# Transfers in source order through the scan and output stages of a parallel-head layer

## The chip, the cores and the metric

The kernel runs on one core of a Trainium2 chip. The metric is the device time of one execution in microseconds (us); lower is better. Several executions are timed and the median is taken; one more execution is profiled, and every row below comes from that one. Engines are named as in the profile: PE multiplies matrices (PEld are its weight loads), DVE, ACT and POOL work on vectors, and SP issues the DMA transfers of this kernel from one in-order queue.

## What is computed

One layer of a diffusion backbone for 128 context tokens and 2048 latent tokens (T = 2176), width 1024, all in float32. The layer normalises and modulates x, projects it, runs a short gated convolution on one half of the channels and a bidirectional mLSTM scan (4 heads of 128) on the other, projects back, adds to x, and ends with a feed-forward part. Cut to what this change touches:

```
h = rmsnorm(x, norm1) * (1 + scale1) + shift1
z = h @ w_in                                   # sc_b, sc_c, sc_x, q, k, v, o, gates
y_sc = sc_b * conv3(sc_c * sc_x)               # short gated convolution
h_m, C, n, m = mlstm_bidir(q, k, v, gates, C0, n0, m0)   # chunks of 128 tokens, two directions
h_m = h_m * rsqrt(mean(h_m**2) + EPS) * mh_norm * sigmoid(o)
x = x + gate1 * (concat(y_sc, h_m) @ w_out)
h2 = rmsnorm(x, norm2) * (1 + scale2) + shift2
up = conv3(h2 @ w_up); a, gg = split(up)
x = x + gate2 * ((silu(gg) * a) @ w_down)
y = rmsnorm(x, final_norm)
```

## The kernel before

Activations lie channels on partitions, tokens along the row. The 2176 tokens are cut into six blocks (BL), five of 384 and one of 256 tokens; blocks 0, 1, 2 are BA, blocks 3, 4, 5 are BB. Every float32 operand of a product is split into a rounded part and a remainder (names ending in H and L, or wh and wl), and a tile of a product takes three matmuls per 128 channels: `gemm` (L201) issues 24 of them, eight each at L206, L207, L208, into one of three accumulator banks. `load_w` (L107) brings a weight tile of 512 KB into a staging tile (`wst`, two buffers, L109), ACT makes wh (L111) and DVE makes wl in two halves (L114); wh and wl have four buffers.

`apply` (L168) normalises and modulates one block: `spread` (L134) puts the per-token factor on all partitions in the one PSUM bank `st`, then for each of eight tiles DVE multiplies (L177), ACT adds the shift and rounds (L181, L185, L186), and DVE forms the remainder (L182, L187). Three pairs of h buffers rotate over the blocks.

The stages, in source order:

1. Start: modulation, block 3, then value and gate products (`vg`, L378) and all projections of BB. With the o projection of BB by block, the h of blocks 0, 1 and 2 is made, each after the four heads that free its buffer (L624 to L626).
2. `vg` of BA (L926): for each block two halves of the columns, three chunks each, 24 matmuls per group (L388 to L390); ACT writes the values (L393), DVE adds the gate bias (L395), which is the last reader of the accumulator. Then the gate phase, woven with the k heads.
3. The scan, in two runs of `weave` (L909). `Sums` units collect state sums per chunk and head pair, `Mix` units compute the outputs. In iteration i the loop traces the first part of unit i, the third part of unit i-3, the second part of unit i-1, the loads of unit i+2, and then one or two steps of a generator `fill` (none in some iterations). The fill (L948) is a chain: q heads and o heads of BA (12 steps each), the short convolution of BA (36 steps), and the output projection of block groups (0, 1) and (2, 3) (16 steps each).
4. What is left of the fill, the sums for the feed-forward part, the output projection of blocks 4 and 5, and the feed-forward part.

In `heads` (L406) a step is one gemm, its eviction by ACT (L403) and the store of the row (L404); the first statement for each head is `load_w`, traced in the step of that head's first block. In `shortconv` (L420) the three weights of a channel tile are loaded in the step of its first gemm; each third step stores a row (L444). In `out_proj` (L451) the two blocks of a group are loaded and split at the group's start (L459 to L462), then for each of eight tiles and each of the two blocks: gemm, DVE multiplies by the gate and adds x (L488), the row is stored (L490), ACT squares it (L497), DVE adds the square up one step later (L498). At the group's end `inv_rms` (L122) sums over partitions with small matmuls (L128) in the bank `st`, DVE scales (L131), POOL takes the power (L132).

In a Mix unit the second product operand R is a 512 KB broadcast from DRAM (L839). The first part multiplies q and k into the one bank S (L850), DVE adds the mask to R (L851), ACT takes exponentials (L855), DVE multiplies S and R (L859), which frees S. The second part loads o2 (L770 via L864), multiplies with the state and values (L873, L875). The third part transposes into the bank `st` (L902), DVE multiplies with o2 (L904), which frees the bank, and o2 is stored (L907). Unit loads are k and q (L770), v (L775), R and sb (L843).

What sets the order on each engine is the planner of the tile framework. It takes the program in source order, simulates it with its own cost model, and issues on each engine what is ready first there, the earlier in the source first among the ready. So a load can be issued long before the place in the source where it is written, as soon as a buffer is free. The finished queue of each engine runs strictly in order on the chip, SP's too.

Of the kernel before, what the change touches and what calls it, by code (L numbers as in the profile page):

```python
# [2 lines left out]

# [7 lines left out]
F32 = mybir.dt.float32  # L11
# [46 lines left out]
def hymba_kernel(ctx: ExitStack, tc: tile.TileContext, I, O):  # L58
# [92 lines left out]
    def rcol(b):  # L151
        t0, n = BL[b]
        return rc[:, t0 // P:(t0 + n) // P]
# [12 lines left out]
        return ss  # L166

    def apply(b, xt, norm):  # L168
        t0, n = BL[b]
        rb = spread(rcol(b), n)  # L170
        hH, hL = h_pair()
        sh = 0 if norm == 0 else 24
        for k in range(KT):
            x = xt[k // 4][:, k % 4]
            for a, e, v in spans(t0, t0 + n):
# [8 lines left out]
                else:  # L184
                    S.activation(x[:, a:e], x[:, a:e], AF.Identity, bias=sv)  # L185
                    S.activation(hH[:, k, a:e], x[:, a:e], AF.Copy)  # L186
                    V.tensor_sub(hL[:, k, a:e], x[:, a:e], hH[:, k, a:e].bitcast(F32))  # L187
        return hH, hL
# [8 lines left out]
    def accumulator():  # L197
        pool = pa[next(turn_a) % len(pa)]
        return pool.tile([P, 512], F32, name="acc")

    def gemm(w, h, n):  # L201
        (wh, wl), (hH, hL) = w, h
        acc = accumulator()
        for k in range(KT):
            w_h, w_l = wh[:, k * P:(k + 1) * P], wl[:, k * P:(k + 1) * P]
            PE.matmul(acc[:, :n], w_h, hH[:, k, :n], start=(k == 0), stop=False)  # L206
            PE.matmul(acc[:, :n], w_h, hL[:, k, :n], start=False, stop=False)  # L207
            PE.matmul(acc[:, :n], w_l, hH[:, k, :n], start=False, stop=(k == KT - 1))  # L208
        return acc


# [142 lines left out]
    with ExitStack() as ph1:  # L354
# [89 lines left out]
                    Q.dma_start(yD[m][:, t0:t0 + n], yr[:, :n])  # L444
                    yield

        def stats(grp, sss):
            for b, ss in zip(grp, sss):
                inv_rms(ss, BL[b][1], rcol(b))

        def out_proj(grps, defer=None):  # L451
            for grp in grps:
                ys, sss = [], []
                for b in grp:
                    t0, n = BL[b]
                    yH, yL = h_pair()
                    for kh in range(2):
                        yt = xp.tile([P, 4, 384], F32, name="xt")
                        Q.dma_start(yt[:, :, :n], yD[4 * kh:4 * kh + 4, :, t0:t0 + n].rearrange("k p t -> p k t"))  # L459
                        for k in range(4):  # L460
                            S.activation(yH[:, 4 * kh + k, :n], yt[:, k, :n], AF.Copy)
                            V.tensor_sub(yL[:, 4 * kh + k, :n], yt[:, k, :n], yH[:, 4 * kh + k, :n].bitcast(F32))  # L462
                    ys.append((yH, yL))
                    sss.append(ssp.tile([P, 384], F32, name="ss"))

                def load_r(m):
                    xs_ = []
                    for b in grp:
                        t0, n = BL[b]
                        xr = rp.tile([P, 384], F32, name="row")  # L470
                        Q.dma_start(xr[:, :n], I["x"][m][:, t0:t0 + n])
                        xs_.append(xr)
                    return xs_

                ws = [load_w(I["w_out"][m]) for m in range(2)]
                nx, pend = load_r(0), []
                for m in range(KT):
                    w, xs_ = ws.pop(0), nx
                    if m + 1 < KT:
                        nx = load_r(m + 1)  # L480
                    if m + 2 < KT:
                        ws.append(load_w(I["w_out"][m + 2]))
                    for b, y, ss, xr in zip(grp, ys, sss, xs_):
                        t0, n = BL[b]
                        acc = gemm(w, y, n)
                        for a, e, v in spans(t0, t0 + n):
                            a, e = a - t0, e - t0
                            V.scalar_tensor_tensor(xr[:, a:e], acc[:, a:e], modT[:, 16 + m, v:v + 1], xr[:, a:e],  # L488
                                                   op0=ALU.mult, op1=ALU.add)
                        Q.dma_start(xD[m][:, t0:t0 + n], xr[:, :n])  # L490
                        while pend:
                            pend.pop()()
                        if m == 0:
                            S.activation(ss[:, :n], xr[:, :n], AF.Square)
                        else:
                            sq = sqp.tile([P, 384], F32, name="sq")
                            S.activation(sq[:, :n], xr[:, :n], AF.Square)  # L497
                            pend.append(lambda ss=ss[:, :n], sq=sq[:, :n]: V.tensor_add(ss, ss, sq))  # L498
                        yield
                while pend:  # L500
                    pend.pop()()
                if grp is grps[-1] and defer is not None:
                    defer.append(lambda: stats(grp, sss))
                else:
                    stats(grp, sss)


        hs = {}
        with tc.tile_pool(name="start", bufs=1, side="right") as stp, \
# [316 lines left out]
        class Mix:  # L826
# [71 lines left out]
            def third(self):  # L898
# [7 lines left out]
                t0 = (c + 1) * P  # L906
                Q.dma_start(yD[4 + 2 * hp:6 + 2 * hp, :, t0:t0 + P].rearrange("h d t -> d h t"), o2)  # L907

        def weave(units, fill, blocks):  # L909

            n = len(units)
            for i in range(-1, n + 3):
                if 0 <= i < n:
                    units[i].first()
                if 0 <= i - 3 < n:
                    units[i - 3].third()
                if 0 <= i - 1 < n:
                    units[i - 1].second()
                for x in (0, 1) if i < 0 else (i + 2,):
                    if x < n:  # L920
                        units[x].load()
# [19 lines left out]
        for hp in range(2):  # L941
            sb = ml.tile([P, 2, 2, 129], F32, name="sb", bufs=5)
            Q.dma_start(sb[:, :, 1, :], I["state"][:, 1, 2 * hp:2 * hp + 2, :])
            sbs.append(sb)
            sf = mb.tile([P, 2, 129], F32, name=f"sf{hp}")
            Q.dma_start(sf, I["state"][:, 0, 2 * hp:2 * hp + 2, :])
            sfs.append(sf)
        fill = chain(heads(BA, hs, 12, qD, AF.Copy, QS), heads(BA, hs, 20, oD, AF.Sigmoid, 1.0),  # L948
                     shortconv(BA, hs), out_proj(((0, 1), (2, 3))))
# [11 lines left out]
        late = []  # L961
        last = out_proj(((4, 5),), late)
        run(islice(last, 1))
        for _ in sums(0, fpool, (1,), (6, 0)):
            run(islice(last, 1))
# [343 lines left out]
```

## Time and profile before

| | us |
|---|---|
| median of 3 runs | 2507.28 |
| the 3 runs | 2504.99, 2507.28, 2508.83 |
| the profiled execution | 2504.05 |
| its span, first to last instruction | 2502.2 |
| busy: PE | 2454.3 |
| busy: DVE | 1731.5 |
| busy: ACT | 1100.3 |
| busy: POOL | 62.9 |

The mean granted PE clock is 0.992 of full speed. Busy times are unions of an engine's instructions; matmuls overlap, so a busy PE is not PE at its peak, and the number of matmuls in a window says more. A wait is written as the waiting instruction, the one that released it, the total, the count and the longest. In rows of single instructions the first number is the start in us from the span's start, the second the duration; brackets hold the idle time of the engine before it and its releaser. SPq rows are DMA issues; the duration is that of the issue, and the landing comes later. By the map of the stages in time: value and gate products of BA begin at about 382 us, the scan's sums at about 500 us, its mixing at about 651 us, the output projection at about 835 us.

### The profile page before, as it was taken

How to read it: one execution, taken by the hardware profiler on the slowest of the kernel's cores; microseconds unless marked ns; L12 is line 12 of the kernel's file. 1: busy time of each engine (PE TensorE's matmuls, PEld its weight loads, DVE VectorE, ACT ScalarE, POOL GpSimd, SP SyncE). 2: the span in 40 equal slices, each digit the busy share in tenths (PEclk: the TensorE clock that was granted, in tenths of full speed). 3: DMA queues.
4: the chain of work that ended last, by engine and by line, in shares of the span. 5: the costliest groups of instructions: out<-in, count | busy, mean ns of one | idle time of the engine just before them, and what ended most of it. 6: DMA issues, size and time to landing. Idle time of an engine off the chain costs nothing.

```text
span 2502.2 us, 44204 instructions
## 1 busy us (share of the span) xinstructions
PE 2454.3 (98%) x17043; PEld 2398.2 (96%) x17043; DVE 1731.5 (69%) x3327; ACT 1100.3 (44%) x2109; POOL 62.9 (3%) x128
## 2 busy tenths in 40 slices
PE   8999999999999989999999999999999999999998
PEld 7999999999999989999999999999999988889998
DVE  4895443433467777789888888776767788677665
ACT  4511133333334444455455445554545454443343
POOL 0000000000011111000000000000000000000000
PEclk9999999999999999999999999999999999999999
DMA  8798723466567886877456446644454476576544
GB/s 276 264 288 257 251 93 112 136 204 205 183 198 213 250 276 198 279 253 259 149 196 217 144 161 212 219 147 168 146 168 147 164 269 233 191 272 207 183 154 151
DMA packets 252437, 506.18 MB, mean 202 GB/s; under 512 B 22962, under 2 KB 153154, under 8 KB 241346
## 3 DMA queue, kind: packets, MB, share of 16 engines
q1 hardware_dynamic: 252226, 503.35, 60.9%
q8 instruction: 134, 2.20, 0.4%
q14 instruction: 77, 0.63, 0.1%
HBM read 355.24 MB, written 148.03 MB: 201 GB/s over the span
## 4 chain that ended last, share of the span: by engine, by line
PE 79%; DMA 8%; DVE 8%; issue 1%; ACT 1%; SPq 1%; POOL 0%; DVEq 0%; ACTq 0%; POOLq 0%
PE pa L1148 7%; PE pa L1150 7%; PE pa L1149 7%; PE acc L206 6%; PE acc L208 6%; PE acc L207 6%; PE pb L1150 4%; PE pb L1148 3%; PE pb L1149 3%; DVE jk L560 3%; PE pa L1206 3%; PE pa L1207 3%; PE pa L1208 3%; DMA wD<-wm 2%; PE pc L1208 2%; PE pc L1206 2%
## 5 line engine op out<-in xcount | busy, mean ns | idle before, releaser
L206 PE MATMUL acc<-hH,wh 128*128 128x384 f32 (+1 forms) x1536 | 514.9, 335 | 5.5 <-DVE cr L430 4.1
L208 PE MATMUL acc<-hH,wl 128*128 128x384 f32 (+1 forms) x1536 | 505.9, 329 | 0.5 <-DVE wl L114 0.5
L207 PE MATMUL acc<-hL,wh 128*128 128x384 f32 (+1 forms) x1536 | 504.9, 329 | 0.0
L1148 PE MATMUL pa<-tH,wh 128*128 128x272 f32 x1408 | 408.5, 290 | 3.8 <-DVE row L488 2.7
L1150 PE MATMUL pa<-tH,wl 128*128 128x272 f32 x1408 | 407.2, 289 | 0.0
L1149 PE MATMUL pa<-tL,wh 128*128 128x272 f32 x1408 | 405.1, 288 | 0.0
L278 ACT ACTIVATE wh<-st 128x512 fp32r<-128x512 f32 (+1 forms) x312 | 189.0, 609 | 403.1 <-PE pa L1149 108.7
L206 PEld LDWEIGHTS acc<-hH,wh 128*128 128x128 f32 x1536 | 291.1, 190 | 8.0 <-DVE cr L430 4.7
L208 PEld LDWEIGHTS acc<-hH,wl 128*128 128x128 f32 x1536 | 290.9, 189 | 1.2 <-DVE wl L114 0.9
L207 PEld LDWEIGHTS acc<-hL,wh 128*128 128x128 f32 x1536 | 291.1, 190 | 0.7
L989 DVE SCALAR_TENSOR_TENSOR tt<-raw,fw,tt 128x127 f32<-128x127 f32 (+4 forms) x264 | 242.3, 947 | 49.3 <-ACT tt L995 48.2
L1148 PEld LDWEIGHTS pa<-tH,wh 128*128 128x128 f32 x1408 | 264.9, 188 | 4.8 <-DVE row L488 2.9
L279 DVE TENSOR_TENSOR wl<-st,wh 128x512 fp32r<-128x512 f32 (+1 forms) x312 | 205.4, 660 | 91.3 <-ACT wh L278 87.9
L1149 PEld LDWEIGHTS pa<-tL,wh 128*128 128x128 f32 x1408 | 265.4, 188 | 0.0
L1150 PEld LDWEIGHTS pa<-tH,wl 128*128 128x128 f32 x1408 | 264.7, 188 | 0.0
L1148 PE MATMUL pb<-tH,wh 128*128 128x272 f32 x704 | 203.6, 289 | 0.4 <-ACT wh L278 0.4
L1150 PE MATMUL pb<-tH,wl 128*128 128x272 f32 x704 | 203.6, 289 | 0.0
L1149 PE MATMUL pb<-tL,wh 128*128 128x272 f32 x704 | 202.7, 288 | 0.0
L278 ACT ACTIVATE wh<-s 128x512 fp32r<-128x512 f32 x176 | 110.9, 630 | 146.5 <-PE pc L1149 90.1
L114 DVE TENSOR_TENSOR wl<-wst,wh 128x512 fp32r<-128x512 f32 (+1 forms) x160 | 105.9, 687 | 64.2 <-ACT wh L111 64.2
L279 DVE TENSOR_TENSOR wl<-s,wh 128x512 fp32r<-128x512 f32 x176 | 120.7, 687 | 29.0 <-ACT wh L278 25.4
L1148 PEld LDWEIGHTS pb<-tH,wh 128*128 128x128 f32 x704 | 132.4, 188 | 0.6 <-ACT wh L278 0.6
(236 smaller groups left out, 5222.0 us busy)
## 6 DMA issues: line engine op xcount, KB each, us to landing
st<-in_w_up SPq DMA_DIRECT2D x88, 512.0 KB, 4.6
wst<-in_w_in SPq DMA_DIRECT2D x48, 512.0 KB, 4.1
wU<-s SPq DMA_DIRECT2D x22, 1024.0 KB, 6.5
s<-wU SPq DMA_DIRECT2D x22, 1024.0 KB, 5.7
st<-wD SPq DMA_DIRECT2D x32, 704.0 KB, 5.2
st<-in_w_down SPq DMA_DIRECT2D x28, 704.0 KB, 4.0
R<-nD SPq DMA_DIRECT2D x34, 512.0 KB, 5.4
wm<-in_w_modr SPq DMA_DIRECT2D x32, 512.0 KB, 3.7
```

Source lines behind the costliest of these rows:

```text
L114: V.tensor_sub(wl[:, a:a + n // 2], st[:, a:a + n // 2], wh[:, a:a + n // 2].bitcast(F32))
L206: PE.matmul(acc[:, :n], w_h, hH[:, k, :n], start=(k == 0), stop=False)
L207: PE.matmul(acc[:, :n], w_h, hL[:, k, :n], start=False, stop=False)
L208: PE.matmul(acc[:, :n], w_l, hH[:, k, :n], start=False, stop=(k == KT - 1))
L278: S.activation(wh[:, :n], a, AF.Copy)
L279: V.tensor_sub(wl[:, :n], a, wh[:, :n].bitcast(F32))
L989: V.scalar_tensor_tensor(o, i, w, o, op0=ALU.mult, op1=ALU.add)
L1148: PE.matmul(acc, wh[:, w], rh, start=(kk == 0 and i in (0, 1, 5)), stop=False, skip_group_check=True)
L1149: PE.matmul(acc, wh[:, w], rl, start=False, stop=False, skip_group_check=True)
L1150: mm = PE.matmul(acc, wl[:, w], rh, start=False, stop=(kk == 3), skip_group_check=True)
L1206: PE.matmul(acc[p], wh[:, k], th[:, t], start=(c == kk == 0), stop=False, skip_group_check=True)
L1208: PE.matmul(acc[p], wl[:, k], th[:, t], start=False, stop=(c == 2 and kk == nk - 1), skip_group_check=True)
```

## The change

- **Ties.** A context `queued()` notes the last SP instruction traced so far and, at its end, adds to each SP instruction traced inside it an ordering edge (no semaphore) behind that one. In `weave` three kinds of pieces run inside such a context: the first and third parts; the second part with the loads of unit i+2; each single step of the fill. The edges order the issue only, between pieces; within a piece the planner stays free. `heads` and `shortconv` themselves are not changed.
- **Output projection.** It becomes one sequence of 48 steps over three groups. Each group runs its first two tiles for the first block and then for the second, then tiles 2 to 5 in pairs, then the last two tiles for the first block and then for the second. `load_y` loads and splits one block in five portions, started at fixed steps: blocks 0 and 1 inside the short convolution, blocks 2 to 5 at output steps 4, 13, 23 and 30. `load_o` asks for the next output weight that is not loaded, when a weight has been used for the last time in a group. Rows of x are loaded three steps ahead.
- **Statistics.** `inv_rms` of a block is traced two steps after its last tile, its matmuls ordered behind the current gemm; only block 5 is left for later instead of blocks 4 and 5.
- **Third block.** The apply of block 2 becomes a generator that advances by one tile behind each value group of `vg`; its x tiles are loaded where the whole apply stood.

```diff
     def apply(b, xt, norm):
+        hH, hL = h_pair()
+        run(apply_to(hH, hL, b, xt, norm))
+        return hH, hL
+
+    def apply_to(hH, hL, b, xt, norm):
         t0, n = BL[b]
         rb = spread(rcol(b), n)
-        hH, hL = h_pair()
...
+            yield
...
+        GROUPS = ((0, 1), (2, 3), (4, 5))
+        STEPS = [(m, b) for a, z in GROUPS for m, b in
+                 [(0, a), (1, a), (0, z), (1, z)] + [(m, b) for m in range(2, 6) for b in (a, z)]
+                 + [(6, a), (7, a), (6, z), (7, z)]]
+        NEXT_Y = {4: 2, 13: 3, 23: 4, 30: 5}
...
+        def load_y(b):
+
+            t0, n = BL[b]
+            ys[b] = yH, yL = h_pair()
+            yt = []
+            for kh in range(2):
+                y = xp.tile([P, 4, 384], F32, name="xt")
+                Q.dma_start(y[:, :, :n], yD[4 * kh:4 * kh + 4, :, t0:t0 + n].rearrange("k p t -> p k t"))
+                yt.append(y)
+            yield
+            for k in range(KT):
+                y = yt[k // 4][:, k % 4, :n]
+                S.activation(yH[:, k, :n], y, AF.Copy)
+                V.tensor_sub(yL[:, k, :n], y, yH[:, k, :n].bitcast(F32))
+                if k % 2:
+                    yield
+
+        def load_o(x):
+            while x < len(STEPS) and STEPS[x][0] in wo:
+                x += 1
+            if x < len(STEPS):
+                wo[STEPS[x][0]] = load_w(I["w_out"][STEPS[x][0]])
...
+                while due and due[0][0] <= x:
+                    b1 = due.pop(0)[1]
+                    with tc.issue_after(latest[0].ins):
+                        inv_rms(sss[b1], BL[b1][1], rcol(b1))
...
+                if m == KT - 1:
+                    due.append((x + 2, b))
+                if b % 2:
+                    wo.pop(m)
+                    load_o(x + 1)
+                if x in NEXT_Y:
+                    prep = chain(prep, load_y(NEXT_Y[x]))
+                next(prep, None)
+                yield
...
-                hs[b] = make_h(b, I["x"], 0)
+                if b < 2:
+                    hs[b] = make_h(b, I["x"], 0)
+                else:
+                    hs[b] = h_pair()
+                    third = apply_to(*hs[b], b, load_x(b, I["x"], xp, "xt", 2), 0)
...
+        @contextmanager
+        def queued():
+
+            traced = nc.cur_bb.bb.instructions
+            n = len(traced)
+            last = next(i.name for i in reversed(traced) if i.engine == mybir.EngineType.SP)
+            yield
+            for i in traced[n:]:
+                if i.engine == mybir.EngineType.SP:
+                    tc.add_manual_dep(i, last, mybir.DependencyInfo(
+                        mybir.DependencyClass.NoSync, mybir.DependencyReason.DATA), reason="queued")
+
         def weave(units, fill, blocks):
 
             n = len(units)
             for i in range(-1, n + 3):
...
+                with queued():
+                    if 0 <= i < n:
+                        units[i].first()
+                    if 0 <= i - 3 < n:
+                        units[i - 3].third()
+                with queued():
+                    if 0 <= i - 1 < n:
+                        units[i - 1].second()
+                    for x in (0, 1) if i < 0 else (i + 2,):
+                        if x < n:
+                            units[x].load()
                 for _ in range(blocks[i % 3]):
-                    next(fill, None)
-
-
-        run(vg(BA, hs, load_vg(0) + load_vg(1)))
+                    with queued():
+                        next(fill, None)
+
+
+        run(vg(BA, hs, load_vg(0) + load_vg(1)), third)
+        run(third)
...
+        def before_out():
+
+            prep = iter(())
+            for x, _ in enumerate(shortconv(BA, hs)):
+                if x in (29, 32):
+                    prep = chain(prep, load_y((x - 29) // 3))
+                if x in (31, 34):
+                    load_o(0)
+                next(prep, None)
+                yield
+            run(prep)
+
         fill = chain(heads(BA, hs, 12, qD, AF.Copy, QS), heads(BA, hs, 20, oD, AF.Sigmoid, 1.0),
-                     shortconv(BA, hs), out_proj(((0, 1), (2, 3))))
+                     before_out(), islice(outs, 32))
```

More of the change, by code (lines that the diff above doesn't have):

```diff
@@ L207, in gemm @@
             PE.matmul(acc[:, :n], w_h, hL[:, k, :n], start=False, stop=False)
-            PE.matmul(acc[:, :n], w_l, hH[:, k, :n], start=False, stop=(k == KT - 1))
+            mm = PE.matmul(acc[:, :n], w_l, hH[:, k, :n], start=False, stop=(k == KT - 1))
+        latest[:] = [mm]
         return acc
@@ L445, in shortconv @@
                     yield
[L447 to L499, printed above, removed]
@@ L508, in hymba_kernel @@
+                if m == KT - 1:
[7 more added lines that the diff above has]
+                yield
+            while pend:
+                pend.pop()()
+            defer.append(lambda: [inv_rms(sss[b1], BL[b1][1], rcol(b1)) for _, b1 in due])
         hs = {}
@@ L960, in hymba_kernel @@
         fp = ph2.enter_context(tc.tile_pool(name="fp", bufs=1, side="right"))
-        late = []
-        last = out_proj(((4, 5),), late)
+        last = outs
         run(islice(last, 1))
```

49 lines of the change are left out of this document (35 added, 14 removed).

## Prediction

> **What bounds the kernel now.** I read the page first (engines, then DMA sizes), then the waits of TensorE (PE), then stage windows, and last the rows of single instructions.
>
> ```profile
> span 2502.2 us, 44204 instructions
> PE 2454.3 (98%) x17043; PEld 2398.2 (96%) x17043; DVE 1731.5 (69%) x3327; ACT 1100.3 (44%) x2109; POOL 62.9 (3%) x128
> wst<-in_w_in SPq DMA_DIRECT2D x48, 512.0 KB, 4.1
> R<-nD SPq DMA_DIRECT2D x34, 512.0 KB, 5.4
> ```
>
> PE is busy for 2454.3 of 2502.2 us. No edit here takes a matmul away, so whatever is won is PE idle time and the slow clock behind it; any new PE wait adds to the time at once. The profiled execution took 2504.05 us, 1.85 over its span and 3.2 below the median of 2507.28. The next two fences are the waits of PE and windows of 25 us (PE busy, weight loads, DVE, ACT, POOL, each with its count; then granted clock, DMA share, GB/s), with two long stretches last.
>
> ```profile
> PE S L850 <- DVE R L859: 5.1, 2, 4.6
> PE st L128 <- DVE o L904: 4.4, 1, 4.4
> PE acc L388 <- DVE gates L395: 3.9, 1, 3.9
> PE pa L1148 <- DVE row L488: 2.7, 1, 2.7
> ```
>
> ```profile
> 375.00:400.00 25.00, 21.06 (x157) 20.87 (x156) 17.18 (x36) 13.63 (x27) 0.30 (x3) 0.86 0.61 186
> 400.00:425.00 25.00, 25.00 (x209) 25.00 (x208) 1.74 (x11) 3.48 (x9) 0.81 (x8) 1.00 0.14 47
> 825.00:850.00 25.00, 25.00 (x168) 25.00 (x168) 21.65 (x60) 13.85 (x40) 4.12 (x6) 1.00 0.79 241
> 875.00:900.00 25.00, 20.36 (x130) 20.04 (x129) 19.51 (x59) 10.11 (x30) 2.40 (x4) 0.89 0.85 274
> 900.00:925.00 25.00, 25.00 (x160) 25.00 (x160) 16.57 (x50) 10.33 (x33) 3.31 (x6) 0.97 0.90 276
> 925.00:950.00 25.00, 20.44 (x101) 19.81 (x100) 17.43 (x55) 12.10 (x32) 4.22 (x6) 0.80 0.84 269
> 1075.00:1100.00 25.00, 21.77 (x164) 21.13 (x162) 17.00 (x29) 13.09 (x22) 1.92 (x2) 1.00 0.92 316
> 490.00:640.00 150.00, 149.76 (x844) 142.82 (x843) 51.91 (x116) 53.97 (x155) 0.00 (x0) 1.00 0.69 210
> ```
>
> Three waits of about 4 us carry the idle time that the change can touch, and each is followed by a lowered clock. The sums of the scan (490 to 640) are the opposite: 149.76 of 150 us busy, nothing to win, everything to lose.
>
> **What the three waits are worth.** *Value blocks (375 to 400).* 157 matmuls where the next window has 209: (209-157)/209 x 25 = 6.2 us lost, 3.9 idle and 2.3 slow clock. *L859 (875 to 925).* Against 168 matmuls, 130 and 160 are 5.7 + 1.2 = 6.8 us lost, 4.6 idle and 2.2 clock. *L904 (925 to 950).* Matmul records are missing, so I go by the clock: 0.80 over 25 us is 10 us at half speed, at most 5.0 lost, with 4.4 idle 9.4. With the second L850 wait (0.5) all that can go is 22.9 us. L1148 stands after the last output tile and stays.
>
> **Third block between value blocks.** The apply of block 2 (six spread matmuls, per tile a product L177, ScalarE copies and L187 or L182) leaves the head of the DVE queue and goes one tile behind each of the first eight value groups.
>
> ```profile
> 393.25 0.55 DVE L187 TENSOR_TENSOR hL<-xt,hH 128x384 fp32r<-128x384 f32 x1
> 393.72 0.70 DVE L114 TENSOR_TENSOR wl<-wst,wh 128x528 fp32r<-128x528 f32 x1
> 394.34 0.30 DVE L395 TENSOR_TENSOR gates<-acc,bgate 128x8 f32<-128x8 f32 x3
> ```
>
> Now three gate additions wait behind all of the apply and free three accumulators at once, at 394.34. After the change each comes behind one tile. The last half of a value weight (L114, to 394.42) is in the same queue and is needed by the fourth group, so I keep 1 us back: -5.2. The two x loads stay ahead of the value blocks. Block 2 is wanted by the thirteenth group, four groups after its last tile; that work covers the move.
>
> **Statistics, output blocks, output weights.** The statistics' matmuls (three per full block, as before) wait for the one st bank, which L904 reads. Now they stand straight behind the scan's matmuls; afterwards they follow an output tile's 24 matmuls, which are cover for L904; ss was finished a tile earlier. Their DVE scaling and POOL power move with them, and the sums that read the result come after the scan. I take the whole 9.4. The two loads, eight copies and eight subtractions per output block are the same work in four portions; output weights are still eight loads per group, now asked for about two tiles before use instead of when a buffer is free. That is near what a load needs (below), and missed in the four places inside the scan where a group begins or reaches its third weight: 0 to 3 us each, I take 2 in all.
>
> **Order on the transfer queue (SP).** In the output stage a broadcast R was issued at 886.71 and the DVE sat before the addition that reads it:
>
> ```profile
> 886.71 0.42 SPq L839 DMA_DIRECT2D R<-nD  x1
> 892.11 0.69 DVE L851 TENSOR_TENSOR R<-R,maskN 128x512 f32<-128x512 f32 x1 [4.50 <-DMA R<-nD]
> 892.72 0.74 DVE L488 SCALAR_TENSOR_TENSOR row<-acc,modT,row 128x128 f32<-128x128 f32 x2
> ```
>
> The eviction L488 and then L859 queued behind it. Tied, each R is issued two scan steps before use; DVE order is still the planner's, so of 6.8 + 0.5 I count 5.4. Together these edits give -5.2 - 9.4 - 5.4 + 2 = -18.
>
> Now the price. The ties hold for every fill in the scan, and there the weights of heads and short convolution are loaded by the same step that uses them (load_w as its first statement, no load ahead). Today the planner moves these loads forward:
>
> ```profile
> 499.72 0.33 SPq L109 DMA_DIRECT2D wst<-in_w_in  x1
> 511.01 0.37 SPq L770 DMA_DIRECT2D k<-kD  x1
> 513.10 0.40 SPq L775 DMA_DIRECT2D v<-vD  x1
> 527.66 1.06 ACT L111 ACTIVATE wh<-wst 128x1024 fp32r<-128x1024 f32 x1 [3.77 <-PE acc L207]
> ```
>
> Counted in order, the load issued at 499.72 is the one converted at 527.66: 28 us of lead. Tied, the load of the next head stands behind the row store (L404) of the last tile, and that store waits for the tile's matmuls and its eviction. SP holds everything behind it: the k and v of the coming unit, then the weight. PE's next tile waits for the weight.
>
> ```profile
> 491.23 0.49 ACT L403 ACTIVATE row<-acc 128x384 f32<-128x384 f32 x1 [4.54 <-PE acc L208]
> 491.75 0.33 SPq L404 DMA_DIRECT2D kD<-row  x1
> L114 DVE TENSOR_TENSOR wl<-wst,wh x36: 673/683/694, 498.4 to 783.7; 128x512 fp32r<-128x512 f32 x36
> 503.83 0.38 PE L792 MATMUL S<-ident,k 128*128 128x128 f32 x2
> 506.24 0.53 PE L206 MATMUL acc<-hH,wh 128*128 128x384 f32 x1
> ```
>
> Per head: eviction and store 0.85 (491.23 to 492.08), k and v 0.77, landing 4.1, conversion 1.06, first half of the remainder 0.68: 7.5 us. PE has scan units meanwhile; two of them fill 503.83 to 506.24, 2.4. That leaves 5 us, seven times (four q heads and four o heads, the first with nothing to wait for): 35.
>
> Four sets of short-convolution weights follow, three of them in the scan's second half, where the queue between a finished tile and a weight is longer:
>
> ```profile
> 678.02 0.33 SPq L444 DMA_DIRECT2D yD<-yr  x1
> 679.14 0.37 SPq L907 DMA_DIRECT2D yD<-o  x1
> 682.11 0.42 SPq L843 DMA_DIRECT2D sb<-sD  x1
> 675.12 0.60 PE L850 MATMUL S<-q,k 128*128 128x128 f32 x4
> 677.49 0.43 PE L206 MATMUL acc<-hH,wh 128*128 128x384 f32 x1
> ```
>
> From the tile's store (678.02) past the output store, R and the rest to the end of sb's issue are 4.5 us. Eviction 0.9, queue 4.5, landing 4.1, conversion 1.06 and 0.68 are 11.2, less one unit's 2.4 on PE: 8.8, or 7 where the next tile is in the same step; I take 8, four times: 32.
>
> All eleven outlast the 3.9 us after which the clock fell, so each costs 2.2 more (the two rows above): 24. Together 35 + 32 + 24 = 91, against 18 won: +73. 2504.05 + 73 = 2577, with 3.2 for the median **2580 us**.
>
> The bounds of one wait: low, two more units pulled forward make 2.6 per head, and below that length the clock held (the 2.7 us before L1148, clock 1.00 at 1075 to 1100); 5 per set with 1.7 of clock. 7 x 2.6 + 4 x 6.7 = 45, less 22.9: +22, 2529. High, the slowest exposed load:
>
> ```profile
> 669.71 0.33 SPq L109 DMA_DIRECT2D wst<-in_w_in  x1
> 676.50 1.04 ACT L111 ACTIVATE wh<-wst 128x1024 fp32r<-128x1024 f32 x1
> ```
>
> 6.8 instead of 4.1: 7 x 7.7 + 4 x 10.7 + 11 x 5 (the ten half-speed microseconds of 925 to 950) = 152, with 10 won: +142, 2649.
>
> The Trainium skill ("TensorE: Matmul & The Clock Gate", The HAM clock gate) states that about 3.4 us of idle halve the clock until a busy window of about 3.4 us has passed. By it a stall would cost 1.7 us of clock, 19 in all, and the time would be 2575; this trace's windows hold 7 and 10 us at half speed, so the rows go before the page.
>
> The Trainium skill ("DMA: Bandwidth & Descriptors", Anatomy of one DMA) also says that a transfer's semaphore wait takes place on the issuing sequencer before dispatch. It speaks against this change; in this trace L404 is issued within 0.03 us of its eviction's end, which agrees but does not prove it.
>
> **Rivals.** *The ties only cure.* If weights still arrive ahead, because the ties do not hold those loads back or the stores before them are never late, the three waits go and nothing comes: 2507 less 18 to 23, 2484 to 2489. For: the 28 us of lead. Against: the load is traced inside the tied step. It decides at a lead of 7.5 us before the previous head's last matmul. 0.11. *Scan units fill the waits*, the low bound: PE takes later units while it waits, 2520 to 2545. For: units need only k and v. Against: those are tied two steps ahead too. 0.15. *The queue is held longer*: of the three short-convolution loads the third waits for a staging buffer (two exist) and holds R and k behind it, so units stall too; above 2655. 0.05. *Neither*: gains and waits cancel within 0.2%, about what a measurement of this kernel can tell from no change. 0.03.
>
> **How the numbers follow.** Forecast 0.66, with 2545 to 2655. The range takes in the rival just below it: 2520 to 2655, 0.81. Faster is the first rival, 0.11; same 0.03; slower 0.66 + 0.15 + 0.05 = 0.86.
>
> **What would show it.** PE waits named L206 or L208 behind ACT wh L111 or DVE wl L114, about eleven, 4 to 9 us, between 500 and 780; clock near 0.9 in those windows; L109 issued right behind a row store; a conversion some 5 to 7 us after its issue, not 28. No waits L395 and L904 of 4 us. I am wrong if L109 keeps leads of 20 us or PE stays above 149 of 150 us busy in the scan's sums.

## The result and the profile after

The changed kernel is slower: 2589.88 us (median of 4 runs, 2586.94 to 2596.28) against 2506.14 us of the kernel before on the same chip (4 runs, 2504.01 to 2508.83). The ratio is 1.035, 95% interval 1.0324 to 1.0376. The forecast was 2580, range 2520 to 2655. The profiled execution of the changed kernel took 2592.02 us.

First the page of the changed kernel: the span, the busy engines, and the loads of projection weights and of R with the size of each and the median time (us) from issue to landing.

```profile
span 2590.1 us, 44059 instructions
PE 2489.3 (96%) x17043; PEld 2415.4 (93%) x17043; DVE 1736.2 (67%) x3327; ACT 1106.5 (43%) x2109; POOL 69.9 (3%) x128
...
wst<-in_w_in SPq DMA_DIRECT2D x48, 512.0 KB, 5.4
R<-nD SPq DMA_DIRECT2D x34, 512.0 KB, 5.4
```

The matmuls are the same 17043. The span is 87.9 us longer, PE's busy time 35.0; the rest, 52.9, is idle time. A busy time that grows with the same matmuls points to the clock: each lasts longer. The mean granted clock fell from 0.992 to 0.981. The share missing from full speed, 0.019 of 2590.1 us, less 0.008 of 2502.2 us before, gives an estimate of 29 us, most of the 35.0. Next the waits of PE in the changed kernel (total, count, longest).

```profile
PE acc L212 <- ACT wh L111: 31.7, 19, 6.4
PE y L836 <- DVE vw L829: 22.3, 13, 3.8
PE y L906 <- DVE hv L916: 3.0, 5, 1.4
```

L212 is the first matmul of `gemm` (L206 before). The waits at L395 and L904 that stood in this list before are gone, and so is the 4.6 us at L859. Two new ones lead: tiles that wait for their weight, as forecast, and scan units that wait for `vw`, the product made from a v that has just landed, which the forecast did not have. The sizes are not those of the forecast: only two of the waits for a weight are over 4 us (6.4 at 686.68 and 5.2 at 934.18), where about eleven of 4 to 9 us were expected. Three windows of the changed kernel follow (behind 500 us the same times no longer hold the same work as before):

```profile
375.00:400.00 25.00, 25.00 (x210) 25.00 (x209) 15.01 (x37) 12.15 (x26) 0.61 (x6) 1.00 0.58 189
525.00:550.00 25.00, 19.52 (x92) 16.80 (x91) 7.07 (x17) 6.70 (x19) 0.00 (x0) 0.86 0.38 114
490.00:640.00 150.00, 122.76 (x590) 107.36 (x588) 42.22 (x94) 40.37 (x111) 0.00 (x0) 0.90 0.46 139
```

The value blocks now run through (210 matmuls where 157 stood). The sums of the scan, 844 matmuls in 150 us before, hold 590: 122.76 us busy, and a clock of 0.90, which over 150 us is 30 us at half speed.

Where the 87.9 us lie can be read from stores that both kernels make: the last row of the first q head, the last row of the fourth o head, the last row of the short convolution, the last row of the output stage. Transfer issues of the kernel before, then of the changed one:

```profile
512.08 0.32 SPq L404 DMA_DIRECT2D qD<-row  x1
634.92 0.32 SPq L404 DMA_DIRECT2D oD<-row  x1
832.58 0.39 SPq L444 DMA_DIRECT2D yD<-yr  x1
1084.05 0.32 SPq L490 DMA_DIRECT2D xD<-row  x1
```

```profile
502.73 0.32 SPq L411 DMA_DIRECT2D qD<-row  x1
679.92 0.32 SPq L411 DMA_DIRECT2D oD<-row  x1
904.71 0.33 SPq L451 DMA_DIRECT2D yD<-yr  x1
1168.50 0.32 SPq L509 DMA_DIRECT2D xD<-row  x1
```

Seven heads took 122.8 us and take 177.2 (+54.4); the short convolution 197.7 and 224.8 (+27.1); the output stage 251.5 and 263.8 (+12.3); all else, span less these three, 1930.2 and 1924.3 (-5.9). The sum is 87.9.

What each stage lost shows in windows with the same bounds: heads, short convolution and output stage of the changed kernel, then the output stage of the kernel before.

```profile
502.73:679.92 177.19, 146.22 (x691) 127.92 (x689) 46.73 (x100) 45.52 (x123) 0.00 (x0) 0.88 0.44 134
679.92:904.71 224.79, 208.06 (x1278) 204.55 (x1277) 129.53 (x392) 83.75 (x241) 22.43 (x36) 0.96 0.60 184
904.71:1168.50 263.79, 243.50 (x1528) 239.15 (x1526) 195.25 (x530) 121.65 (x302) 26.67 (x37) 0.96 0.82 265
```

```profile
832.58:1084.05 251.47, 238.98 (x1517) 237.13 (x1515) 188.96 (x519) 114.02 (x292) 22.13 (x36) 0.97 0.82 259
```

PE is idle for 31.0 us in the heads and for 16.7 in the short convolution (before, for 0.0 in both), and for 20.3 in the output stage (before 12.5). All 22.3 us of the waits behind vw lie in the heads. The waits for weights, in the heads and then in the output stage:

```profile
PE acc L212 <- ACT wh L111: 4.5, 7, 0.9
```

```profile
PE acc L212 <- ACT wh L111: 16.6, 7, 5.2
```

So of the 31.7 us that tiles wait for weights only 4.5 lie in the heads. There PE waits mostly in scan units.

How one head loses its time, from the timeline of the changed kernel:

```profile
502.21 0.49 ACT L410 ACTIVATE row<-acc 128x384 f32<-128x384 f32 x1 [3.90 <-PE acc L214]
502.73 0.32 SPq L411 DMA_DIRECT2D qD<-row  x1
503.14 0.39 SPq L803 DMA_DIRECT2D k<-kD  x1
503.63 0.43 SPq L854 DMA_DIRECT2D sD<-sb  x1
504.12 0.42 SPq L808 DMA_DIRECT2D v<-vD  x1
504.59 0.44 SPq L109 DMA_DIRECT2D wst<-in_w_in  x1
...
509.24 1.11 PE L836 MATMUL y<-vw,kT 128*128 128x258 f32 x4 [2.51 <-DVE vw L829]
510.12 1.05 ACT L111 ACTIVATE wh<-wst 128x1024 fp32r<-128x1024 f32 x1
...
511.22 0.69 PE L212 MATMUL acc<-hH,wh 128*128 128x384 f32 x1 [0.88 <-ACT wh L111]
```

The eviction of the head's last tile (502.21) releases the row store, and behind it in the queue go k, the state store, v, and only then the weight. 9.0 us after the eviction's start PE begins the next tile. It took scan units meanwhile, but their v (504.12) stood behind the same store, and so PE waited 2.51 us inside the cover too.

### The profile page after: what moved, and what is told of

Same layout as the page of the kernel before. It is cut to its first block, busy times and chain, and to the rows that moved or that the text cites. A ratio compares the mean times of both kernels' runs of the same rounds, so it can differ in the third digit from the quotient of the medians.

```text
span 2590.1 us, 44059 instructions
## 1 busy us (share of the span) xinstructions
PE 2489.3 (96%) x17043; PEld 2415.4 (93%) x17043; DVE 1736.2 (67%) x3327; ACT 1106.5 (43%) x2109; POOL 69.9 (3%) x128
## 4 chain that ended last, share of the span: by engine, by line
PE 74%; DMA 11%; DVE 8%; ACT 2%; issue 2%; SPq 2%; POOL 1%; DVEq 0%; ACTq 0%; POOLq 0%
PE pa L1211 7%; PE pa L1213 7%; PE pa L1212 7%; PE acc L212 6%; PE acc L213 5%; PE acc L214 5%; PE pb L1213 3%; PE pb L1211 3%; PE pb L1212 3%; PE pa L1269 2%; PE pa L1270 2%; PE pa L1271 2%; DVE jk L589 2%; DMA wD<-wm 2%; PE pc L1211 2%
## 5 line engine op out<-in xcount | busy, mean ns | idle before, releaser
L212 PE MATMUL acc<-hH,wh 128*128 128x384 f32 (+1 forms) x1536 | 521.0, 339 | 36.8 <-ACT wh L111 31.7
L213 PE MATMUL acc<-hL,wh 128*128 128x384 f32 (+1 forms) x1536 | 512.5, 334 | 0.0
L212 PEld LDWEIGHTS acc<-hH,wh 128*128 128x128 f32 x1536 | 298.5, 194 | 45.1 <-ACT wh L111 38.7
L213 PEld LDWEIGHTS acc<-hL,wh 128*128 128x128 f32 x1536 | 297.0, 193 | 0.3 <-issue 0.2
```

## Experiments

The table gives each kernel's median, its ratio to the kernel before with the 95% interval (the kernel before, timed beside them, had medians of 2503.2 to 2504.6), and the stage times of its profiled execution, read from the same four stores (us). One execution can lie some us off the median (4.3 below it in 7, 6.7 above it in 10), so stage differences of that size say little.

| | median | ratio | heads | short conv. | output | all else |
|---|---|---|---|---|---|---|
| before | | | 122.8 | 197.7 | 251.5 | 1930.2 |
| after | 2589.88 | 1.035 (1.0324 to 1.0376) | 177.2 | 224.8 | 263.8 | 1924.3 |
| 1 weights untied | 2501.27 | 0.9987 (0.9973 to 1.0001) | 124.6 | 201.6 | 249.8 | 1926.0 |
| 2 only weights tied | 2510.44 | 1.0024 (1.0009 to 1.0040) | 122.9 | 209.2 | 251.6 | 1923.0 |
| 3 weights earlier | 2515.73 | 1.0044 (1.0031 to 1.0058) | 122.4 | 208.9 | 260.9 | 1925.2 |
| 4 output weights too | 2511.53 | 1.0021 (1.0010 to 1.0032) | 122.4 | 209.8 | 252.3 | 1924.9 |
| 5 k and v untied | 2525.00 | 1.0087 (1.0070 to 1.0105) | 122.0 | 225.3 | 255.9 | 1920.7 |
| 6 ties alone | 2611.23 | 1.0432 (1.0410 to 1.0455) | 174.9 | 225.2 | 271.5 | 1936.7 |
| 7 no ties | 2496.23 | 0.9974 (0.9963 to 0.9985) | 122.8 | 198.4 | 247.4 | 1921.6 |
| 8 third block alone | 2498.34 | 0.9981 (0.9970 to 0.9993) | 122.8 | 197.3 | 249.6 | 1925.8 |
| 9 no ties, own bank | 2495.66 | 0.9964 (0.9952 to 0.9976) | 122.8 | 199.1 | 249.4 | 1923.5 |
| 10 and a fifth R | 2490.49 | 0.9954 (0.9937 to 0.9970) | 122.8 | 198.3 | 244.6 | 1929.6 |
| 11 third block, own bank | 2498.37 | 0.9976 (0.9964 to 0.9988) | 122.8 | 198.3 | 252.9 | 1924.8 |
| 12 third block, fifth R | 2500.69 | 0.9990 (0.9976 to 1.0004) | 122.8 | 198.5 | 251.5 | 1928.5 |

**1. Weight loads without ties.** `load_w` notes its transfers, and `queued` leaves them out:

```diff
-        Q.dma_start(st[:, :n], src)
+        wst_loads.add(Q.dma_start(st[:, :n], src).ins.name)
...
-                if i.engine == mybir.EngineType.SP:
+                if i.engine == mybir.EngineType.SP and i.name not in wst_loads:
```

> The changed kernel with one thing undone: the loads of weight tiles (load_w, in the fill of the scan) carry no ordering edge, all other transfers keep theirs. My theory (the price is the weight loads tied behind the row stores of the tiles before them): the TensorE waits of gemm behind ACT wh and DVE wl between 500 and 1100 us go, those of the scan units behind vw with them, and 90 to 105 us of the 2590 go: 2485 to 2505, the head's load issued over 20 us before its conversion. Rival A (the price is the ties on the scan units' own loads, k, v, R and o2 held behind stores): nothing changes there, above 2560. Rival B (the price is the new output stage itself): the 25 to 30 us lost after 900 us stay, 2515 or more.

Measured 2501.27: 88.6 of the 2589.88 us go with this one class of transfer. Heads are back at 124.6, while k and v keep their ties there. In this kernel's window of the sums PE is busy again, at full clock:

```profile
490.00:640.00 150.00, 148.66 (x837) 141.32 (x836) 52.74 (x116) 58.22 (x151) 0.00 (x0) 1.00 0.64 194
```

Its waits of PE name neither wh L111 nor vw. So the waits for v were a consequence: the units came under PE early only because the weight was missing. Rivals A and B fall. (At the few steps whose last transfer is a weight load, three-weight steps of the short convolution and output steps, the pieces behind it are tied to a free load; the heads have no such step.)

**2. Only the weight loads tied.** The complement:

```diff
+                if i.engine == mybir.EngineType.SP and i.name in wst_loads:
```

> The complement of the kernel with untied weights: only the loads of weight tiles keep their ordering edges, the units' loads, row stores, output stores and all else carry none. My theory: the waits of gemm behind ACT wh stay, about one per head and per short-convolution set, 2560 to 2600; k and v may now overtake the stores, so the waits of the second unit product behind vw may go and take some 10 us with them. Rival A: 2490 to 2515.

Measured 2510.44, as rival A had it. But this kernel did not hold what it was meant to hold, as experiment 5 showed, and no more is read from it.

**3. The same ties, weights earlier in the source.** `heads` asks for the next head's weight in the step of its second block; `shortconv` for the next set in its fifth, eighth and ninth step:

```diff
+        ahead = []
...
+        def ask(o):
+            ahead.append(load_w(I["w_in"][o]))
...
-                w = load_w(I["w_in"][w0 + h])
+                w = ahead.pop(0) if then else load_w(I["w_in"][w0 + h])
                 for b in blocks:
+                    for o in then[h].get(b, ()) if then else ():
+                        ask(o)
...
+                    if more and b == blocks[1]:
+                        ask(4 + m + 1)
+                    if more and b == blocks[2]:
+                        ask(8 + m + 1)
...
+                    if more and b == blocks[2]:
+                        ask(0 + m + 1)
```

> The changed kernel with every tie kept, but the weight loads of heads and short convolution written earlier in the source: the next head's weight in the step of the head's second block, the next short-convolution set over the last steps of the set before it. My theory: each load is then issued two or three tiles (16 us or more) before its use, and the losses of heads and short convolution (about 70 to 80 us with their slow clock) go; the output weights are as late as before, so their 25 to 30 us stay: 2505 to 2525. Rival A: the units' loads are tied as before, above 2560. Rival B: as the theory, since it puts the rest on the output stage; this run shows how much that is.

Measured 2515.73, inside the expected 2505 to 2525. All ties stand, k and v are held as in the changed kernel, and the heads take 122.4 us:

```profile
490.00:640.00 150.00, 150.00 (x850) 143.60 (x849) 55.09 (x120) 54.73 (x148) 0.00 (x0) 1.00 0.66 197
```

A tie by itself costs the heads nothing; a weight written in the step that uses it, once tied, costs 7.8 us per head. What is left of the waits for weights in this kernel, against the next:

```profile
PE acc L212 <- ACT wh L111: 15.0, 7, 5.3
```

**4. One output weight more.** Experiment 3 with a third `load_o` at output step 0; from there three weights are held.

```diff
+                if x == 0:
+                    load_o(0)
                 if b % 2:
                     wo.pop(m)
                     load_o(x + 1)
```

> The kernel with earlier weights of heads and short convolution, and in the output stage one weight more held (a third load_o at output step 0, so each later one is asked for one weight earlier; four buffers exist). My theory: the waits behind output weights inside the tied part go as well, 2484 to 2500, faster than the kernel before by 0.3 to 0.9%. Rival B (the new order of the output stage costs by itself, not its weights): no gain over the run without the third weight, 2505 to 2525.

```profile
PE S L905 <- DVE R L914: 5.6, 3, 4.0
...
PE acc L212 <- ACT wh L111: 1.8, 2, 1.0
```

The waits for weights, nearly all of them for output weights, went from 15.0 to 1.8 us and the output stage from 260.9 to 252.3, but the time, 2511.53, is no gain on the kernel before; I had expected 2484 to 2500. The short convolution stays 12 us over before. In it PE is idle for 6.0 us, and no run shows where the rest comes from. The longest wait at S behind R (4.0 us, at 838.26) stands just behind its last row (835.67), in the output stage; R follows below.

**5. k and v without ties.** The loads of k2 and v2 are left out of `queued`, all else is tied.

```diff
+            d = Q.dma_start(t, src[2 * hp:2 * hp + 2, :, c * P:(c + 1) * P].rearrange("h p t -> p h t"))
+            if name == "k2":
+                free.add(d.ins.name)
...
+            free.add(Q.dma_start(v2, vD[c][:, 2 * hp:2 * hp + 2]).ins.name)
...
+                if i.engine == mybir.EngineType.SP and i.name not in free:
```

> The changed kernel with one thing undone: the loads of k and v of the scan units carry no ordering edge; weight loads, row stores, R, q, o2 and all else keep theirs. Two kernels so far say that weights free gives 2501 and weights alone tied gives 2510, so a late weight is not dear by itself. Theory now: a weight behind the row store costs what scan units can't cover, and they cover it only if their k and v are not behind the same store. Expected then 2510 to 2535: the waits of the second unit product behind vw go, those of gemm behind ACT wh shrink from 31.7 us to under 12, heads take almost nothing between 500 and 680, short-convolution sets and output weights keep 10 to 25 us. Rival (it is the stores, R, q or o2 in order, or the planner's order itself): 2560 or more, as k and v change nothing there.

Measured 2525.00, in the range expected, yet not for the reason expected. `queued` ties to the last SP instruction traced, and ahead of a head's step that is the v load of a unit, here free itself. So the weight of the head was not held behind the row store. From this kernel's transfers:

```profile
507.57 0.42 SPq L411 DMA_DIRECT2D qD<-row  x1
...
510.25 0.43 SPq L109 DMA_DIRECT2D wst<-in_w_in  x1
...
513.99 0.42 SPq L411 DMA_DIRECT2D qD<-row  x1
...
519.33 0.39 SPq L411 DMA_DIRECT2D qD<-row  x1
```

The three rows are those of one head, and the next head's weight is issued between the first and the second, 9 us ahead of the last row. Experiment 2 has the same flaw. What the kernel does show: the first short-convolution set's weights are issued at 625.40, right behind the last o row at 624.24, as in the changed kernel, and the short convolution takes 225.3 us against 224.8 there. With k and v free the sets cost as much. Whether units with their data at hand would cover a head's late weight stays open; a kernel that ties to the last held transfer was not tried.

**6. The ties alone on the kernel before**, `queued` and the new `weave`, with nothing else of the change:

```diff
+                with queued():
+                    if 0 <= i < n:
+                        units[i].first()
...
+                    with queued():
+                        next(fill, None)
```

> The kernel before with nothing but the ties (the three contexts in weave); output stage, statistics and third block as before. Theory: the price of weights and units behind one store is all here, 85 to 100 us, and the old output stage adds some 5 to 20 because it loads both blocks of a group in one tied step: 2590 to 2625, no less than 2580. Rival (the new output stage or its weights carry the price): under 2550.

Measured 2611.23. Heads 174.9 and short convolution 225.2 as in the changed kernel: the price of these two stages is in the ties over their generators alone. The old output stage adds 20.0 to its 251.5. I put that down to the two blocks of a group that it loads in one tied step, which no run shows by itself. In these two executions the new output stage, 263.8, is the shorter of the two under ties.

**7. No ties**, the changed kernel with the edge never added:

```diff
-                if i.engine == mybir.EngineType.SP:
+                if False:
```

> The changed kernel without any tie: third block between value blocks, new output sequence and statistics stay. Theory: 6 us of the third block for sure, of the 9.4 of the statistics at most half, since with weights free the wait for the one bank st came back at another place (2.6 and 2.4 us and 13.7 us of slow clock near 925): 2494 to 2501. Rival (ties are what keeps the bank's wait away): 2503 to 2510, with R or st waits of 4 us as before.

**8. Third block alone**, the kernel before with `apply_to` and its advance behind the value groups:

```diff
-        run(vg(BA, hs, load_vg(0) + load_vg(1)))
+        run(vg(BA, hs, load_vg(0) + load_vg(1)), third)
+        run(third)
```

> The kernel before with nothing but the third block between value blocks. Theory: the 375 to 400 window gives back its 6 us and the rest of the time stays as it was: 4 to 7 us faster than before, ratio 0.9972 to 0.9984. Rival (what is won there is lost later, as the planner's order behind it changes): no change within 0.1%.

Measured 2496.23 and 2498.34, both as the theory had it. The third block gives 6.3 us (2504.6 less 2498.34). The new output stage with its statistics adds about 2 more by the medians, but the two intervals overlap, so that gain is not shown. Waits of PE in 7, without ties:

```profile
PE st L128 <- DVE o L937: 2.9, 1, 2.9
PE st L935 <- DVE rc L131: 2.2, 1, 2.2
PE S L883 <- DVE R L892: 2.0, 1, 2.0
```

The statistics wait for the bank st as before, only elsewhere.

**9. The statistics in an accumulator bank**, no ties:

```diff
-        ps = pst.tile([P, 512], F32, name="st")
+        ps = bank() if bank else pst.tile([P, 512], F32, name="st")
...
-                        inv_rms(sss[b1], BL[b1][1], rcol(b1))
+                        inv_rms(sss[b1], BL[b1][1], rcol(b1), accumulator)
```

> The kernel without ties, and the statistics' sums in the output stage go into one of the three accumulator banks instead of the bank st. Theory: without ties the statistics still waited for st (2.9 us behind L937, 2.2 us behind L131, 10.2 us at half speed after them), because L937 stood in the DVE queue behind an R that landed late; with a bank of their own both waits go: 5 to 9 us less than without ties, 2487 to 2492, about 0.6% under the kernel before. Rival (the late R and the DVE queue are the cause, the bank only the place where it is seen): PE waits at S or y behind DVE instead, 2494 to 2499.

**10. And a fifth buffer for R:**

```diff
-            v2 = ml.tile([P, 2, 129], F32, name="v2", bufs=5)
+            v2 = ml.tile([P, 2, 129], F32, name="v2", bufs=4)
...
-                self.R = mb.tile([P, 2, 2, 2, P], F32, name="R", bufs=4)
+                self.R = mb.tile([P, 2, 2, 2, P], F32, name="R", bufs=5)
...
-                    sj = mb.tile([P, P], F32, name="sj", bufs=2)
+                    sj = mb.tile([P, P], F32, name="sj", bufs=1)
```

> The kernel without ties and with the statistics' own bank, and a fifth buffer for R (four before; v2 gives up its fifth, sj its second, for the space). Theory: R is issued one unit earlier, DVE's wait for it (3 us near 907) and TensorE's wait S behind R (2.0 us near 881) shrink: 2 to 5 us less than with the bank alone. Rival (the queue, not the buffer, sets when R is issued, or the missing v2 and sj buffers cost as much): within 2 us of the run with the bank alone, or slower.

**11. Third block and own bank**, experiment 8 with the bank of 9 in the old output stage:

```diff
-                    stats(grp, sss)
+                    stats(grp, sss, accumulator)
```

> The kernel before with the third block between value blocks and the statistics' sums of blocks 0 to 3 in an accumulator bank; output stage and queue as before. Theory: the statistics' wait for st (4.1 us behind the product with o2, 6.8 us at half speed after it) goes without any move of the statistics: 5 to 8 us less than the third block alone, 2490 to 2494. Rival (the wait comes back at S or y behind DVE): 2496 to 2499, no gain.

**12. Third block and fifth R**, experiment 8 with the three buffer counts of 10.

> The kernel before with the third block between value blocks and a fifth buffer for R (v2 gives up its fifth, sj its second); queue, output stage, statistics and the bank st as before. Theory now: both waits between 875 and 950, the one at S and the one of the statistics at st, come from an R that lands late and holds the DVE queue; a fifth buffer alone takes both away: 4 to 9 us less than the third block alone, 2489 to 2494. Rival (the statistics' wait needs its move or its own bank, or the new output sequence): the wait of 4 us at st stays, 2495 to 2499.

The waits of PE in 9, 10, 11 and 12, in this order:

```profile
PE S L883 <- DVE R L892: 8.3, 4, 3.9
```

```profile
PE S L883 <- DVE R L892: 3.2, 3, 1.3
```

```profile
PE S L858 <- DVE R L867: 8.1, 3, 3.5
```

```profile
PE S L858 <- DVE R L867: 5.0, 3, 3.3
...
PE st L128 <- DVE o L912: 4.4, 1, 4.4
```

With a bank of their own the statistics wait no more, and the time comes back at S behind R: 2495.66 against 2496.23, and 2498.37 against 2498.34. The rival was right in both: the bank is where the wait was seen, not what caused it. The fifth R shortened the wait at S in 10, but DVE waits for R in all as long as before (54.2 us in 20 waits, against 47.7 in 20 in experiment 9), so the mechanism I gave is not shown; on the old output stage (12) it gave nothing, and the wait at st stayed there, as the rival had it. The intervals of 9 and 10 overlap, and the profiled execution of 10 was its slowest, 2497.20 us. The fastest kernel found is 10, no ties, 0.3 to 0.6% under the kernel before.

What holds DVE at this place looks like a matter of placement. For the R that the prediction quotes (issued at 886.71, mask added at 892.11), this is the product that needs it, in the kernel before:

```profile
914.86 0.68 DVE L859 TENSOR_TENSOR R<-S,R 128x512 f32<-128x512 f32 x1
```

R was there over 22 us early. It is the mask addition that the planner put in DVE's queue some 5 us after R's issue, just when it lands, and whatever stands behind it waits. In the changed kernel:

```profile
820.24 0.41 SPq L872 DMA_DIRECT2D R<-nD  x1
...
826.64 0.68 DVE L884 TENSOR_TENSOR R<-R,maskN 128x512 f32<-128x512 f32 x1
...
838.80 0.68 DVE L892 TENSOR_TENSOR R<-S,R 128x512 f32<-128x512 f32 x1
```

18.6 us from issue to product instead of 28.2. Counted in order for the R issued between 780 and 960, the lead was 26 to 32 us before and is 7 to 21 with ties. The ties made R later, and the addition still follows its issue by 5 to 10 us, while the product is much closer. A kernel with the addition ordered behind later work on DVE was not tried, so that the placement costs time, and that moving it would cure the wait, is argued, not shown.

## Why the prediction was right

The sign and the mechanism held: a weight load that stands behind the row store in the tied queue comes too late for the next tile. The sum, +73 on the profiled execution, came out at +87.9. That it came so near is partly luck: the short convolution was put 14 us too high, the output stage 25 us too low, and the two errors offset each other in part. Term by term:

**Heads, 35 and 15 of clock for seven: measured 54.4.** The chain was as drawn, eviction, row store, queue, landing, conversion: 9.0 us from eviction to the next tile, of which 1.5 (503.05 to 504.59) in the queue where I had 0.77, and 5.5 from issue to conversion where I had 4.1; the remainder's 0.68 does not count, since the first matmul needs wh alone. Experiments 1 and 3 take it away in two ways. Of the 54.4, 31.0 are idle time, near the 35, and about 21 are clock (0.12 of 177 us), above the 15. But the idle time stands at another place than forecast. I had the tile wait for its weight; PE took scan units for longer than the 2.4 us that I charged (it was busy for 4.8 of the 9.0 us above), so that a tile of the heads waited 0.9 us at most for its weight, and these scan units were late as well (22.3 us behind vw). The rival "scan units fill the waits" has failed on the objection that I noted.

**Short convolution, 32 and 9 of clock: measured 27.1.** Mis-sized: 16.7 us are idle time where I had 32, and the clock of 0.96 over 225 us is about the 9 that I had. I charged each set a queue of 4.5 us. The second set had just that: from the row store past the unit's o, k, v, q, R and sb,

```profile
732.02 0.32 SPq L451 DMA_DIRECT2D yD<-yr  x1
...
735.65 0.40 SPq L872 DMA_DIRECT2D R<-nD  x1
736.10 0.43 SPq L876 DMA_DIRECT2D sb<-sD  x1
736.57 0.90 SPq L109 DMA_DIRECT2D wst<-in_w_in  x2
```

but the third had 0.4 (792.50 to 792.88, no unit between), the first 1.2 and the fourth 5.4. The rival of the longer queue had its mechanism right: the third load of a set is issued 6.4 to 8.4 us behind the second (in the first set 688.03 behind 681.59), and k, v, q and R of the next unit stand behind it (there 688.46 to 689.87). The time still stayed under its 2655.

**Value blocks, -5.2: measured -6.3 (experiment 8)**, near the 6.2 that the window held.

**Statistics -9.4, R -5.4, output weights +2, together -12.8: measured +12.3.** This is where the prediction failed, and the sum survived because these terms were small beside the ties. The mis-sized term is the output weights: asked for two tiles ahead they are too late once tied, and tiles wait 16.6 us for them, not 2; 13.2 us of waits went when a third was held (experiment 4). The waits that I meant to win did shrink in the changed kernel: in the output stage those at S behind R went from 5.1 to 0.9 us, and the 4.4 us behind L904 went to none. But that is no gain to count on. Where the weights are on time, the waits come back: 5.6 us at S in experiment 4, 2.9 and 2.2 us at st in experiment 7, where the statistics' cover of 24 matmuls did not help, and with a bank of their own 8.3 us at S (experiment 9). "Each R is issued two scan steps before use" was true and no gain: it had been issued earlier still.

**The clock, 2.2 per stall.** In the sums, 30 us at half speed in 150 are 15 us lost over about six heads: 2.5 each. The low bound rested on a stall of 2.7 us that left the clock alone; that does not carry. In experiment 5 PE waited 2.18 us for a weight at 742.85, and behind it stands

```profile
743.00:746.40 3.40, 3.40 (x11) 3.07 (x12) 3.21 (x8) 2.31 (x6) 1.44 (x2) 0.50 0.36 96
```

The Trainium skill ("TensorE: Matmul & The Clock Gate", The HAM clock gate) lets the clock fall after about 3.4 us of idle; this stall was shorter and had 0.32 us of idle before it, so here the measurement decides.

## What to carry to other kernels

Before transfers are tied to source order, go through the source and ask of each load how many steps ahead of its use it is written. A load in the step that uses it is fine under a planner that moves it; under a tie it cost 7.8 us per head here, and what PE took up in the meantime waited behind the same store. When the tie is made to the last transfer traced, see that that transfer is held too. And when an engine waits for data, look up when the result is needed: an R that was 28 us ahead looked late, by the rows above because an addition was placed where it lands.

## What the runs showed that was not expected

Half-speed stretches in the changed kernel are longer than one stall would suggest: 525 to 550 has a clock of 0.86, 7 us at half speed in 25. Work taken up to cover a wait can itself wait for the same queue: 22.3 of the new idle time of PE was in scan units, and it vanished with the weight's tie, though nothing of the units was changed. And taking one wait away on a single bank (experiments 9 and 11) moved 4 to 6 us of PE waiting to the next bank (S: 8.3 against 2.0 in experiment 7, 8.1 against 4.3 in experiment 8) without a gain.
